# Taking the high and the low part of x in one 512-column matmul, in a one-core transformer block

## The chip, the core and the metric

The kernel runs on one core of a Trainium2 chip. The metric is device time in microseconds for one launch: 1659.37 us is the median of three runs of the kernel before (1657.81 to 1660.90 us).

The core has five engines that run side by side and wait for one another through semaphores: PE (TensorE, the matrix products; "PEld" in the profile is its loading of weights), DVE (VectorE), ACT (ScalarE), POOL (GpSimd) and SP, which here only issues the loads of the large weights. A matmul holds one operand in the array (the weights, 128 rows by up to 128 columns) and streams the other past it (the moving operand, up to 512 columns). Its sums go to PSUM, a memory of 8 banks of 512 floats on each of 128 partitions; DVE and ACT read it and write to SBUF. That reading is called eviction below.

## What is computed

One block of a network on 256 tokens of 2048 channels, in float32 throughout. Cut to the matrix products with the large weights:

```python
h = rms_norm(x);  u = h @ w_in                       # 2048 x 6000, a little over
y = concat(ssd_mixer(u[...]), rwkv7_mixer(u[...]))   # two recurrent mixers
x = x + y @ w_out                                    # 2048 x 2048
h = rms_norm(x);  m = rms_norm(mem)                  # 256 memory tokens
x = x + softmax((h @ wq) (m @ wk).T) (m @ wv) @ wo   # 4 heads of 512
h = rms_norm(x);  x = x + square(relu(h @ w1)) @ w2  # 2048 x 8192 x 2048
return rms_norm(x)
```

## The kernel before

**Products in three parts.** TensorE takes float32 operands in one pass if they are rounded to a shorter mantissa (the type fp32r). To keep float32 accuracy the kernel splits each operand into a high part `hi` (rounded) and a low part `lo` (the rest, rounded), by `split`: ACT writes `hi`, DVE writes `lo = src - hi`. A product w·x then is `whi·xhi + whi·xlo + wlo·xhi`, three matmuls that add into the same PSUM columns.

**A unit.** All large products but one (`wv`) go through `unit`. A unit is 128 output channels (112 and 96 in the first two): 16 tiles of 128 input channels, in two halves of 8. The weights are the operand held in the array, x transposed is the moving one, with 256 tokens as its columns. For each half, lines 197 and 198 run the 8 pairs `whi·xhi`, `whi·xlo` in turn, and line 204 then runs the 8 `wlo·xhi`. That makes 48 matmuls of 256 columns a unit, each with its own weight load; the sum takes 256 of the 512 floats of a bank. There are 240 units: 48 of `w_in`, 16 each of `wk`, `w_out`, `wq` and `wo`, 64 of `w1` and 64 of `w2`. The product with `wv` (lines 856, 858, 859) is laid out the other way about: memory tokens are held in the array and 512 columns of the weights move.

**Weights.** SP issues the load of a half (512 KB) ahead of its use, ACT splits off its `hi` (`L161`, 128x1024), DVE its `lo` (`L162`). In the MLP whole units are loaded (1 MB) and there are two more pairs of buffers for the parts (`wvb` and `wZ` in the names of the rows).

**Eviction.** PSUM is used through two pools: `acc`, three banks for units, and `sm`, five for everything else. One instruction evicts a unit: a DVE product with the norm's factor (`L320`, `L374`, `L379`, `L841`, `L977`), a DVE addition to the residual (`L871`), or a `split` straight from PSUM for the queries.

**Work beside the units.** The two mixers, the memory's norm and the attention are written as generators. `unit` calls `beside` after each quarter of a unit, and `beside` lets them issue some of their instructions. While the 48 units of `w_in` and the first ones of `wk` run, DVE and ACT thus also compute the mixers. The framework's scheduler then fixes the order on each engine; an engine works off its order strictly, an instruction that waits holds up all behind it.

**x in parts.** The split inputs are pairs of tiles, `Ahi`, `Alo` and `Bhi`, `Blo` in the rows (`pair_tiles`), each 16 x 256 floats on a partition. `Bhi` and `Blo` also hold x itself at first, then tensors of the mixers (`ar`, `bk`), then the memory.

Of the kernel before, what the change touches and what calls it, by code (L numbers as in the profile page):

```python
# [18 lines left out]
P = 128  # L19
# [9 lines left out]
# Per-channel vectors, one column of 128 channels each.  # L29
# [12 lines left out]
# Width of each unit of w_in, in the order in which the units are worked on.  # L42
# [28 lines left out]
def trunk(ctx, tc, xT, memT, cpack, w_in, w2, a2, g2, w_out, wq, wk, wv, wo, w1, w2f, outT):  # L71
# [28 lines left out]
    # tri[s, l] = 1 where s <= l; mask[(hh, uv, s), (ar, t)]: s < t for a, s <= t for r.  # L100
# [7 lines left out]
    # Rows for the two parts of a number, so that one product sums them and spreads them over partitions.  # L108
# [18 lines left out]
    # Loads the table that the first norm needs.  # L127
# [14 lines left out]
    # Halves of what goes into a tanh that stands for a sigmoid, and 1 - mu.  # L142
# [48 lines left out]
    def unit(w_u, m, xh, xl, raws=(None, None), interleaved=False):  # L191
        """PSUM [m, T] = (2048 rows of weights, m columns)ᵀ · xᵀ."""
        halves = [load_half(w_u[:, h * 8 * m:(h + 1) * 8 * m], (8, m), raws[h]) for h in range(2)]
        ps = acc.tile([P, 512], F32, name="acc")
        for h, (wh, wl) in enumerate(halves):
            for j in range(8):
                mm(ps[:m, :T], wh[:, j], xh[:, 8 * h + j], start=h + j == 0, stop=False)  # L197
                mm(ps[:m, :T], wh[:, j], xl[:, 8 * h + j], start=False, stop=False)  # L198
                if interleaved:
                    mm(ps[:m, :T], wl[:, j], xh[:, 8 * h + j], start=False, stop=h * j == 7)  # L200
                if j == 5:
                    beside(PER / 4)
            for j in range(0 if interleaved else 8):
                mm(ps[:m, :T], wl[:, j], xh[:, 8 * h + j], start=False, stop=h * j == 7)  # L204
# [16 lines left out]
    def rstd_tokens(sq, width, name):  # L221
        """[token, tile] = 1 / sqrt(sum(sq) / width + eps)."""
# [9 lines left out]
    def over_partitions(r, name, copy=True):  # L232
        """[any partition, token] from [token, tile]."""
# [11 lines left out]
    # ==== 1. norm and input projection ====  # L245
    ah, al = pair_tiles("A")
    xr = big.tile([P, KT, T], F32, name="xr", tag="Bhi")
# [5 lines left out]
    # Work beside the large products: generators that yield the unit they need  # L253
    # next (a tuple), what they have cost (a float), or for how many steps they wait for other engines (an int).
# [3 lines left out]
    def beside(part):  # L258
        """Traces a share of each stream, as far as the finished units allow."""
# [32 lines left out]
    def in_unit(n):  # L292
        m = UNITS[n][2]
        w_u = w_in[uoff[n]:uoff[n] + P * KT * m].rearrange("(p c) -> p c", p=P)
        return unit(w_u, m, ah, al, (raws[:2], (raws[2], None), (None, None))[min(n, 2)], n == 0)

    # What the first unit needs, in the order in which it needs it.
# [7 lines left out]
    for q in range(4):  # L305
        for kt in range(4 * q, 4 * q + 4):
            split(ah[:, kt], al[:, kt], xr[:, kt], col("g_mix", kt))
# [7 lines left out]
    def shifted(out, ps, name, i, m):  # L315
        """out = u + (u of the token before - u) mu, u = ps * rb; out by token, or by chunk and token."""
        u = tp.tile([P, T], F32, name="u")
        mu = col(name, i)[:m]
        with tc.high_priority():
            V.tensor_tensor(u[:m], ps[:m, :T], rb[:m], ALU.mult)  # L320
# [741 lines left out]
```

## Time and profile before

| | |
|---|---|
| median of three runs | 1659.37 us (1657.81 to 1660.90) |
| span of the profiled execution, first to last instruction | 1658.7 us |
| PE busy | 1630.8 us, 13631 matmuls |
| DVE busy | 1011.0 us, 1506 instructions |
| ACT busy | 825.0 us, 1197 instructions |
| POOL busy | 115.7 us |
| read from HBM | 277.34 MB, 169 GB/s over the span |
| mean granted TensorE clock | 0.993 of full speed |

The profiled execution's own time is its span of 1658.7 us and the little that lies around it; the page gives no other figure for it.

Matmuls are pipelined: a row's duration (0.28 us for 256 columns) includes the way through the array, and the next matmul starts long before it ends. What a matmul costs in a stream is therefore read from the distance of the starts, and a PE that is "busy" all the time is not shown by that to be at its limit. Durations of single DVE and ACT instructions overlap slightly in the same way (two of 0.42 us back to back take 0.76 us).

### The profile page before, as it was taken

The numbers are of one execution on the slowest core, as the hardware profiler recorded it, in microseconds if no ns is written. First come the engines' busy times: TensorE is split into PE (matmuls) and PEld (weight loads), VectorE is DVE, ScalarE is ACT, GpSimd is POOL, SyncE is SP. The second block draws the span as 40 slices with busy tenths as digits, with TensorE's granted clock in tenths as the row PEclk, the third lists the DMA queues.
The fourth block names the chain that finished last, engine by engine and source line by source line (L and its number), as shares of the span: only waits on it lengthen the run. The fifth ranks groups of instructions, "written<-read, shape, count | busy, mean of one in ns | idle before, by whom it ended". The sixth has DMA issues, their size and how long they took to land.

```text
span 1658.7 us, 32204 instructions
## 1 busy us (share of the span) xinstructions
PE 1630.8 (98%) x13631; PEld 1592.7 (96%) x13631; DVE 1011.0 (61%) x1506; ACT 825.0 (50%) x1197; POOL 115.7 (7%) x147
## 2 busy tenths in 40 slices
PE   7999999998999999999999999999999999999997
PEld 7999999998998889999999999999999999999997
DVE  6876697889676446655666555455544554455543
ACT  5674445685455445445545554344433543345553
POOL 1011112112000002100011000000000000000011
PEclk9999999999999999999999999999999999999998
DMA  6554455353456665554665555555555555555551
GB/s 190 170 162 146 131 181 161 102 162 105 150 151 209 195 189 184 178 166 141 229 186 164 170 189 181 178 181 188 190 180 178 181 186 190 180 179 181 186 189 55
DMA packets 61040, 282.56 MB, mean 170 GB/s; under 512 B 7456, under 2 KB 8352, under 8 KB 44512
## 3 DMA queue, kind: packets, MB, share of 16 engines
q1 hardware_dynamic: 57312, 272.39, 50.8%
q0 software_dynamic: 3008, 6.03, 1.2%
q8 instruction: 106, 1.74, 0.4%
q10 hardware_dynamic: 576, 2.10, 0.4%
q14 instruction: 38, 0.31, 0.1%
HBM read 277.34 MB, written 3.15 MB: 169 GB/s over the span
## 4 chain that ended last, share of the span: by engine, by line
PE 94%; issue 3%; DVE 1%; DMA 1%; ACT 0%; POOL 0%; SPq 0%; DVEq 0%; POOLq 0%; ACTq 0%
PE acc L197 27%; PE acc L204 27%; PE acc L198 27%; PE acc L858 2%; PE acc L856 2%; PE acc L859 2%; PE sm L478 1%; PE sm L599 1%; DMA raw<-in 1%; PE sm L226 1%; PE sm L896 0%; PE sm L898 0%; PE sm L897 0%; PE sm L395 0%; PE sm L587 0%
## 5 line engine op out<-in xcount | busy, mean ns | idle before, releaser
L197 PE MATMUL acc<-Ahi,hi 128*128 128x256 f32 (+2 forms) x1792 | 450.1, 288 | 8.4 <-ACT hi L161 8.4
L198 PE MATMUL acc<-Alo,hi 128*128 128x256 f32 (+2 forms) x1792 | 445.7, 285 | 1.4 <-DVE Alo L165 1.4
L161 ACT CAST hi<-raw 128x1024 fp32r<-128x1024 f32 (+1 forms) x256 | 267.7, 1046 | 284.8 <-PE acc L198 173.1
L162 DVE TENSOR_TENSOR lo<-raw,hi 128x1024 fp32r<-128x1024 f32 (+1 forms) x256 | 312.0, 1219 | 131.5 <-ACT hi L161 121.8
L197 PEld LDWEIGHTS acc<-Ahi,hi 128*128 128x128 f32 (+2 forms) x1792 | 345.1, 193 | 10.7 <-ACT hi L161 8.4
L198 PEld LDWEIGHTS acc<-Alo,hi 128*128 128x128 f32 (+2 forms) x1792 | 345.2, 193 | 2.8 <-DVE Alo L165 2.1
L197 PE MATMUL acc<-Bhi,hi 128*128 128x256 f32 x1024 | 253.1, 284 | 0.0
L204 PE MATMUL acc<-Ahi,lo 128*128 128x256 f32 (+1 forms) x1776 | 252.5, 284 | 0.0
L198 PE MATMUL acc<-Blo,hi 128*128 128x256 f32 x1024 | 252.2, 283 | 0.0
L204 PEld LDWEIGHTS acc<-Ahi,lo 128*128 128x128 f32 (+1 forms) x1776 | 230.4, 192 | 0.4
L197 PEld LDWEIGHTS acc<-Bhi,hi 128*128 128x128 f32 x1024 | 196.5, 192 | 1.0 <-issue 0.2
L198 PEld LDWEIGHTS acc<-Blo,hi 128*128 128x128 f32 x1024 | 196.6, 192 | 0.1
L204 PE MATMUL acc<-Bhi,lo 128*128 128x256 f32 x1024 | 146.7, 285 | 0.0
L219 POOL TENSOR_TENSOR sq<-sq,t 128x256 f32<-128x256 f32 x50 | 54.8, 1096 | 1181.8 <-ACT t L218 1176.8
L204 PEld LDWEIGHTS acc<-Bhi,lo 128*128 128x128 f32 x1024 | 133.5, 193 | 0.8 <-issue 0.6
L871 DVE TENSOR_TENSOR x<-x,acc 128x256 f32<-128x256 f32 x96 | 40.4, 421 | 150.4 <-PE acc L204 150.4
L198 PE MATMUL acc<-Blo,wvb 128*128 128x256 f32 x512 | 125.7, 283 | 0.0
L197 PE MATMUL acc<-Bhi,wvb 128*128 128x256 f32 x512 | 125.7, 283 | 0.0
L197 PE MATMUL acc<-Ahi,wvb 128*128 128x256 f32 x512 | 125.6, 283 | 0.0
L198 PE MATMUL acc<-Alo,wvb 128*128 128x256 f32 x512 | 125.6, 283 | 0.0
L161 ACT CAST hi<-wK 128x1024 fp32r<-128x1024 f32 x64 | 67.0, 1047 | 92.2 <-PE acc L198 92.2
L161 ACT CAST hi<-wV 128x1024 fp32r<-128x1024 f32 x64 | 67.0, 1047 | 92.0 <-PE acc L198 92.0
(316 smaller groups left out, 2455.2 us busy)
## 6 DMA issues: line engine op xcount, KB each, us to landing
raw<-in SPq DMA_DIRECT2D x252, 512.0 KB, 3.9
wK<-in SPq DMA_DIRECT2D x64, 1024.0 KB, 4.8
wV<-in SPq DMA_DIRECT2D x64, 1024.0 KB, 4.9
xr<-in SPq DMA_DIRECT2D x4, 512.0 KB, 9.1
mr<-in POOLq DMA_DIRECT2D x4, 512.0 KB, 5.6
x<-in ACTq DMA_DIRECT2D x4, 512.0 KB, 5.9
out<-x SPq DMA_DIRECT2D x7, 256.0 KB, 2.4
u<-in POOLq DMA_DIRECT2D x8, 128.0 KB, 3.2
```

Source lines behind the costliest of these rows:

```text
L161: nc.scalar.copy(hi, src)
L162: V.tensor_tensor(lo, src, hi.bitcast(F32), ALU.subtract)
L197: mm(ps[:m, :T], wh[:, j], xh[:, 8 * h + j], start=h + j == 0, stop=False)
L198: mm(ps[:m, :T], wh[:, j], xl[:, 8 * h + j], start=False, stop=False)
L204: mm(ps[:m, :T], wl[:, j], xh[:, 8 * h + j], start=False, stop=h * j == 7)
L219: nc.gpsimd.tensor_tensor(sq, sq, t, ALU.add)
L226: mm(ps[:, i:i + 1], q[:, i * P:(i + 1) * P], ones[:, 0:1], start=k == 0, stop=k == len(sq) - 1)
L478: mm(o[:, c * 64:c * 64 + 64], bk[HH[hh], p, c].rearrange("p k t -> p (k t)"), ar[HH[hh], p, c].rearrange("p k t -> p (k t)"), start=True, ...
L856: mm(pss[i], mh[:, kt, tk], wl[:, j], start=False, stop=kt == KT - 1)
L858: mm(pss[i], mh[:, kt, tk], wh[:, j], start=kt == 0, stop=False)
L859: mm(pss[i], ml[:, kt, tk], wh[:, j], start=False, stop=False)
L871: V.tensor_tensor(x2[:, i], x2[:, i], ps[:, :T], ALU.add)
```

## The change

`unit` takes x as one tile that holds both parts, `x[:, 0]` high and `x[:, 1]` low. The pair `whi·xhi`, `whi·xlo` becomes one matmul of 512 columns: its moving operand is `x[:, :, kt]`, two runs of 256 floats that lie 16 x 256 floats apart, and its output is the whole bank, `whi·xhi` in the left half and `whi·xlo` in the right. The `wlo·xhi` matmuls add to the left half as before. At eviction the halves are summed: `joined` lets ACT copy the right half to SBUF (tile `j`, one buffer) and DVE add the left half to it, and what follows reads `j`; `residual` adds both halves to x2, one after the other. `pair_tile` gives one tile of twice the size, so that `ar` and `bk` share one, too. Comments were taken out, so line numbers move.

```diff
-    def unit(w_u, m, xh, xl, raws=(None, None), interleaved=False):
+    def unit(w_u, m, x, raws=(None, None), interleaved=False):
...
         for h, (wh, wl) in enumerate(halves):
             for j in range(8):
-                mm(ps[:m, :T], wh[:, j], xh[:, 8 * h + j], start=h + j == 0, stop=False)
-                mm(ps[:m, :T], wh[:, j], xl[:, 8 * h + j], start=False, stop=False)
+                kt = 8 * h + j
+                mm(ps[:m].rearrange("p (s t) -> p s t", s=2), wh[:, j], x[:, :, kt], start=kt == 0, stop=False)
                 if interleaved:
-                    mm(ps[:m, :T], wl[:, j], xh[:, 8 * h + j], start=False, stop=h * j == 7)
+                    mm(ps[:m, :T], wl[:, j], x[:, 0, kt], start=False, stop=kt == 15)
...
             for j in range(0 if interleaved else 8):
-                mm(ps[:m, :T], wl[:, j], xh[:, 8 * h + j], start=False, stop=h * j == 7)
+                mm(ps[:m, :T], wl[:, j], x[:, 0, 8 * h + j], start=False, stop=h * j == 7)
...
-    def pair_tiles(tag):
-        return (big.tile([P, KT, T], F32R, name=f"{tag}hi", tag=f"{tag}hi"),
-                big.tile([P, KT, T], F32R, name=f"{tag}lo", tag=f"{tag}lo"))
+    def joined(ps, m=P):
+        t = tp.tile([P, T], F32, name="j", bufs=1)
+        with tc.high_priority():
+            nc.scalar.copy(t[:m], ps[:m, T:])
+            V.tensor_tensor(t[:m], t[:m], ps[:m, :T], ALU.add)
+        return t
+
+    def pair_tile(tag):
+        return big.tile([P, 2, KT, T], F32R, name=f"{tag}pair", tag=tag)
...
-                V.tensor_tensor(xc[:, i], ps[:, :T], rb, ALU.mult)
+                V.tensor_tensor(xc[:, i], joined(ps), rb, ALU.mult)
...
         with tc.high_priority():
-            V.tensor_tensor(x2[:, i], x2[:, i], ps[:, :T], ALU.add)
+            for s in range(2):
+                V.tensor_tensor(x2[:, i], x2[:, i], ps[:, s * T:(s + 1) * T], ALU.add)
...
-            V.scalar_tensor_tensor(t, ps[:, :T], 0.0, rbf, ALU.max, ALU.mult)
+            V.scalar_tensor_tensor(t, joined(ps), 0.0, rbf, ALU.max, ALU.mult)
             act(t, t, AF.Square)
-            split(fh[:, j], fl[:, j], t)
+            split(f_[:, 0, j], f_[:, 1, j], t)
```

On PE, where one half of a unit of `w2` ends and the next begins (`Ahi`, `Alo`, later `Apair`, is x; `hi`, `lo`, `wvb`, `wZ` are parts of weights), there stood before:

```order
L197 MATMUL acc<-Ahi,hi 128x256
L198 MATMUL acc<-Alo,hi 128x256
L204 MATMUL acc<-Ahi,lo 128x256 [waits DVE_49]
L204 MATMUL acc<-Ahi,lo 128x256 x7
L197 MATMUL acc<-Ahi,wvb 128x256 [waits Activation_49]
L198 MATMUL acc<-Alo,wvb 128x256
```

In the same place of the changed kernel stand:

```order
L199 MATMUL acc<-Apair,wvb 128x512 [waits DVE_49,Activation_49]
L199 MATMUL acc<-Apair,wvb 128x512 x7
L205 MATMUL acc<-Apair,wZ_8949 128x256 [waits DVE_49]
L205 MATMUL acc<-Apair,wZ_8949 128x256 x7
L199 MATMUL acc<-Apair,hi 128x512 [waits Activation_49]
```

Sixteen matmuls of 256 columns have become eight of 512; the eight of 256 columns with the low part of the weights are left. The first matmul of a unit now waits for two engines, since both ACT and DVE read the bank that it writes.

On DVE, at the eviction of a unit of `w1` (its norm's product, `t<-acc,rb`, and the split of the result), there stood before:

```order
L162 TENSOR_TENSOR Alo<-t,Ahi 128x256 [waits Activation_49]
L162 TENSOR_TENSOR lo<-wK_10477,hi 128x1024 [waits DVE_49,DMAHW5_49,PE_49,Activation_49]
L977 SCALAR_TENSOR_TENSOR t<-acc,rb 128x256 [waits PE_49]
L162 TENSOR_TENSOR wZ_10476<-wK_10477,wvb 128x1024 [waits DVE_49,Activation_49]
L162 TENSOR_TENSOR Alo<-t,Ahi 128x256 [waits Activation_49]
```

There now stand:

```order
L162 TENSOR_TENSOR lo<-wV_8951,hi 128x1024 [waits PE_49,Activation_49]
L214 TENSOR_TENSOR j<-j,acc 128x256 [waits DVE_49,Activation_49]
L987 SCALAR_TENSOR_TENSOR t<-j,rb 128x256 [waits DVE_49]
L162 TENSOR_TENSOR lo<-wK_8950,hi 128x1024 [waits DMAHW1_49,PE_49,Activation_49]
L162 TENSOR_TENSOR Apair<-t,Apair 128x256 [waits Activation_49]
```

One addition of 128x256 more, and it waits for ACT, whose copy of the right half (`L213 COPY j<-acc`, new in ACT's order) waits for PE.

On PE, near the end of the mixers, where the memory's first units (`Bhi`, later `Bpair`, is the memory in parts) run beside the transposes and the gate (`L631`, `L639`, later `L639`, `L647`), there stood before:

```order
L631 MATMUL sm<-ident,rx 128x128 [waits DVE_49]
L631 MATMUL sm<-ident,rx 128x128 x2
L197 MATMUL acc<-Bhi,hi 128x256
L197 MATMUL acc<-Bhi,hi 128x256 [waits Activation_49]
L198 MATMUL acc<-Blo,hi 128x256
L197 MATMUL acc<-Bhi,hi 128x256
L639 MATMUL sm<-pg,u 128x256 [waits DMASW2_49,Activation_49]
L639 MATMUL sm<-pg,u 128x256
L631 MATMUL sm<-ident,rx 128x128 [waits Activation_49]
```

There now stand:

```order
L199 MATMUL acc<-Bpair,hi 128x512 [waits DVE_49]
L205 MATMUL acc<-Bpair,lo 128x256
L199 MATMUL acc<-Bpair,hi 128x512 [waits DVE_49] x4
L199 MATMUL acc<-Bpair,hi 128x512 [waits Activation_49]
L199 MATMUL acc<-Bpair,hi 128x512 x4
L639 MATMUL sm<-ident,rx 128x128 [waits DVE_49]
L639 MATMUL sm<-ident,rx 128x128 x2
L647 MATMUL sm<-pg,u 128x256 [waits DMASW2_49,Activation_49]
```

More of the memory's first two units now stands ahead of the transposes, and each of its matmuls needs both parts of its tile, where `whi·xhi` needed only the high one.

## Rows read from the trace of the kernel before

**Rows 1.** The page: busy time and share of each engine, then the chain by engine.
```profile
PE 1630.8 (98%) x13631; PEld 1592.7 (96%) x13631; DVE 1011.0 (61%) x1506; ACT 825.0 (50%) x1197; POOL 115.7 (7%) x147
...
PE 94%; issue 3%; DVE 1%; DMA 1%; ACT 0%; POOL 0%; SPq 0%; DVEq 0%; POOLq 0%; ACTq 0%
```

**Rows 2.** Waits of PE: who waited for whom, total us, times, longest us.
```profile
PE acc L197 <- ACT hi L161: 8.4, 1, 8.4
PE sm L729 <- DVE vb L640: 2.4, 1, 2.4
PE sm L639 <- DMA u<-in: 1.7, 2, 0.9
PE sm L226 <- POOL sq L219: 1.6, 2, 0.8
```

**Rows 3.** Busy us (count) of each engine by stretch, then granted clock, DMA share, GB/s.
```profile
33.00:240.00 207.00, 206.51 (x1787) 201.85 (x1786) 157.89 (x284) 115.97 (x186) 23.26 (x32) 0.99 0.52 156
240.00:320.00 80.00, 80.00 (x911) 76.34 (x911) 63.86 (x129) 44.80 (x79) 13.78 (x25) 1.00 0.45 134
320.00:380.00 60.00, 59.94 (x719) 56.45 (x718) 53.55 (x96) 44.59 (x82) 9.26 (x13) 1.00 0.48 153
380.00:412.00 32.00, 27.28 (x182) 24.79 (x181) 29.96 (x57) 19.74 (x34) 8.00 (x8) 0.95 0.30 92
...
912.00:1640.00 728.00, 728.00 (x6069) 728.00 (x6069) 371.95 (x442) 329.09 (x408) 14.44 (x13) 1.00 0.52 177
```

**Rows 4.** PE in order of time, two halves of `w2` meeting: start, duration, line, count.
```profile
1000.11 1.12 PE L204 MATMUL acc<-Bhi,lo 128*128 128x256 f32 x8
1001.07 0.28 PE L197 MATMUL acc<-Ahi,hi 128*128 128x256 f32 x1
1001.19 0.28 PE L198 MATMUL acc<-Alo,hi 128*128 128x256 f32 x1
```

**Rows 5.** PE in order of time, the product with `wv`, 512 columns.
```profile
528.78 1.07 PE L856 MATMUL acc<-lo,Bhi 128*128 128x512 f32 x4
529.69 0.39 PE L858 MATMUL acc<-hi,Bhi 128*128 128x512 f32 x1
...
531.50 1.07 PE L856 MATMUL acc<-lo,Bhi 128*128 128x512 f32 x4
```

**Rows 6.** PE groups by line and form: mean ns of one, idle before.
```profile
L204 PE MATMUL acc<-Ahi,lo 128*128 128x256 f32 (+1 forms) x1776 | 252.5, 284 | 0.0
L204 PE MATMUL acc<-Bhi,lo 128*128 128x256 f32 x1024 | 146.7, 285 | 0.0
L204 PE MATMUL acc<-Bhi,wZ 128*128 128x256 f32 x512 | 71.9, 283 | 0.0
L204 PE MATMUL acc<-Ahi,wZ 128*128 128x256 f32 x512 | 71.9, 283 | 0.0
```

**Rows 7.** PE in order of time, 28 to 30 us.
```profile
28.29 0.41 PE L197 MATMUL acc<-Ahi,hi 128*96 128x256 f32 x1
...
29.79 0.41 PE L198 MATMUL acc<-Alo,hi 128*96 128x256 f32 x1
```

**Rows 8.** As rows 3, the stretch from 28 us.
```profile
28.00:33.00 5.00, 5.00 (x28) 5.00 (x29) 0.68 (x4) 1.50 (x3) 0.00 (x0) 0.58 0.12 47
```

**Rows 9.** DVE and ACT groups by form: count, busy us, mean ns, idle before.
```profile
L871 DVE TENSOR_TENSOR x<-x,acc 128x256 f32<-128x256 f32 x96 | 40.4, 421 | 150.4 <-PE acc L204 150.4
L573 ACT COPY t<-sm 128x256 f32<-128x256 f32 x8 | 3.0, 372 | 2.2 <-PE sm L571 2.1
```

**Rows 10.** DVE in order of time, evictions of `w1` and (back to back) `wk`.
```profile
1542.71 0.42 DVE L977 SCALAR_TENSOR_TENSOR t<-acc,rb 128x256 f32<-128x256 f32 x1 [1.54 <-PE acc L204]
1543.05 1.22 DVE L162 TENSOR_TENSOR lo<-wV,hi 128x1024 fp32r<-128x1024 f32 x1
1544.18 0.42 DVE L162 TENSOR_TENSOR Alo<-t,Ahi 128x256 fp32r<-128x256 f32 x1
...
422.68 0.76 DVE L841 TENSOR_TENSOR kx<-acc,rb 128x256 f32<-128x256 f32 x2 [1.45 <-issue]
```

**Rows 11.** DVE in order of time, the last two evictions of `w_in`.
```profile
379.71 0.42 DVE L374 TENSOR_TENSOR xc<-acc,rb 128x256 f32<-128x256 f32 x1
...
386.74 0.42 DVE L374 TENSOR_TENSOR xc<-acc,rb 128x256 f32<-128x256 f32 x1
```

**Rows 12.** As rows 3, the first ten us of the crowded stretch.
```profile
380.00:390.00 10.00, 9.54 (x76) 9.09 (x74) 10.00 (x20) 7.26 (x12) 1.12 (x2) 1.00 0.47 142
```

**Rows 13.** As rows 3, instructions on the tile `acc` alone, without POOL.
```profile
240.00:320.00 80.00, 56.67 (x441) 53.68 (x441) 3.80 (x9) 0.00 (x0) 1.00 0.45 134
320.00:380.00 60.00, 40.25 (x307) 37.30 (x305) 2.84 (x7) 0.00 (x0) 1.00 0.48 153
380.00:412.00 32.00, 16.86 (x117) 15.54 (x118) 0.56 (x2) 0.00 (x0) 0.95 0.30 92
```

More of the change, by code (lines that the diff above doesn't have):

```diff
@@ L243, in over_partitions @@
         return b
-    ah, al = pair_tiles("A")
-    xr = big.tile([P, KT, T], F32, name="xr", tag="Bhi")
+    a_ = pair_tile("A")
+    xr = big.tile([P, KT, T], F32, name="xr", tag="B")
     uoff, off = [], 0
@@ L294, in in_unit @@
         w_u = w_in[uoff[n]:uoff[n] + P * KT * m].rearrange("(p c) -> p c", p=P)
-        return unit(w_u, m, ah, al, (raws[:2], (raws[2], None), (None, None))[min(n, 2)], n == 0)
+        return unit(w_u, m, a_, (raws[:2], (raws[2], None), (None, None))[min(n, 2)], n == 0)
     raws = []
@@ L335, in trunk @@
     H16 = slice(96, 112)
-    ar = big.tile([P, 8, NCH, 2, C], F32, name="ar", tag="Bhi")
-    bk = big.tile([P, 8, NCH, 2, C], F32, name="bk", tag="Blo")
+    arbk = big.tile([P, 2, 8, NCH, 2, C], F32, name="arbk", tag="B")
+    ar, bk = arbk[:, 0], arbk[:, 1]
     rx = big.tile([P, 16 * T + 8 * NCH], F32, name="rx", tag="X16")
@@ L642, in normed @@
         yield ("xbc", 7)
[L644 removed]
+        y2.append(pair_tile("A"))
         for p in range(8):
[L646 removed]
+            split(y2[0][:, 0, 8 + p], y2[0][:, 1, 8 + p], vb[:, p])
             yield 0.4
@@ L835, in trunk @@
     finish(s_mem)
-    mh, ml, rtm, rbm = m2
+    m_, rtm, rbm = m2
+    mh, ml = m_[:, 0], m_[:, 1]
     kx = big.tile([P, KT, T], F32, name="kx", tag="K16")
     for i in range(16):
-        ps = unit(wk[i], P, mh, ml)
+        ps = unit(wk[i], P, m_)
         with tc.high_priority():
-            V.tensor_tensor(kx[:, i], ps[:, :T], rbm, ALU.mult)
+            V.tensor_tensor(kx[:, i], joined(ps), rbm, ALU.mult)
     finish(s_mix)
-    yh, yl = y2
+    y_, = y2
     vx = big.tile([P, 2, D], F32, name="vx", tag="V16")
@@ L870, in residual @@
         with tc.high_priority():
-            V.tensor_tensor(x2[:, i], x2[:, i], ps[:, :T], ALU.add)
+            for s in range(2):
+                V.tensor_tensor(x2[:, i], x2[:, i], ps[:, s * T:(s + 1) * T], ALU.add)
         if sq is not None:
             square_into(sq, x2[:, i], i == 0)
-    hh_, hl_ = pair_tiles("B")
+    h_ = pair_tile("B")
     sqx = tp.tile([P, T], F32, name="sq")
     for i in range(16):
-        ps = unit(w_out[i], P, yh, yl)
+        ps = unit(w_out[i], P, y_)
         residual(ps, i, sqx)
-        split(hh_[:, i], hl_[:, i], x2[:, i], col("g_x", i))
+        split(h_[:, 0, i], h_[:, 1, i], x2[:, i], col("g_x", i))
     rtx = rstd_tokens([sqx], D, "x")
     V.tensor_scalar(rtx, rtx, 512 ** -0.5, None, ALU.mult)
-    oh, ol = pair_tiles("A")
+    o_ = pair_tile("A")
     qp = big.tile([P, 2, 4, T], F32R, name="qp", tag="Z8")
@@ L942, in trunk @@
     for i in range(16):
-        ps = unit(wq[i], P, hh_, hl_)
+        ps = unit(wq[i], P, h_)
         while i % 4 == 0 and i and ("s", i // 4 - 1) not in done:
@@ L946, in trunk @@
         with tc.high_priority():
-            split(qp[:, 0, i % 4], qp[:, 1, i % 4], ps[:, :T])
+            split(qp[:, 0, i % 4], qp[:, 1, i % 4], joined(ps))
         done.add(("q", i))
     finish(s_att)
-    hh_, hl_ = pair_tiles("B")
+    h_ = pair_tile("B")
     sqx = tp.tile([P, T], F32, name="sq")
     for i in range(16):
-        ps = unit(wo[i], P, oh, ol)
+        ps = unit(wo[i], P, o_)
         residual(ps, i, sqx)
-        split(hh_[:, i], hl_[:, i], x2[:, i], col("g_ffn", i))
+        split(h_[:, 0, i], h_[:, 1, i], x2[:, i], col("g_ffn", i))
     rbf = over_partitions(rstd_tokens([sqx], D, "ffn"), "ffn")
@@ L972, in trunk @@
     for q in range(4):
-        fh, fl = pair_tiles("A")
+        f_ = pair_tile("A")
         for j in range(16):
-            ps = unit(w1[16 * q + j], P, hh_, hl_, whole(w1[16 * q + j]))
+            ps = unit(w1[16 * q + j], P, h_, whole(w1[16 * q + j]))
             t = temp()
-            V.scalar_tensor_tensor(t, ps[:, :T], 0.0, rbf, ALU.max, ALU.mult)
+            V.scalar_tensor_tensor(t, joined(ps), 0.0, rbf, ALU.max, ALU.mult)
             act(t, t, AF.Square)
-            split(fh[:, j], fl[:, j], t)
+            split(f_[:, 0, j], f_[:, 1, j], t)
         for i in range(16):
-            ps = unit(w2f[q, i], P, fh, fl, whole(w2f[q, i]))
+            ps = unit(w2f[q, i], P, f_, whole(w2f[q, i]))
             residual(ps, i, sqx if q == 3 and i < KT - 1 else None)
```

22 lines of the change are left out of this document (10 added, 12 removed).

## The prediction

> **What bounds the kernel now.** I first read the busy shares and the chain of work that ended last [rows 1]. PE is busy for 98% of the span and carries 94% of the chain; DVE carries 1%. A pipelined PE can look busy while it waits, so I then read whom PE waited for [rows 2]: 8.4 us before the first matmul, and after that nothing over 2.4 us. The table of stretches says where another engine comes near [rows 3]. In the MLP, from 912 to 1640 us, DVE is busy for 372 of 728 us. Beside the mixers it climbs: 80% from 240 to 320 us, 89% from 320 to 380 us, and 29.96 of 32 us from 380 to 412 us, the one stretch where PE is plainly idle (27.28 of 32). So the kernel is a stream of matmuls almost from end to end, with one place of 32 us where DVE sets the pace.
>
> **What the change does to the stream.** The price of one matmul is the distance of starts. Eight of 256 columns start within 0.96 us, so one costs 0.120 us [rows 4]. At 2.4 GHz, 256 columns are 0.1067 us, which leaves 0.0133 us that isn't columns. Where 512 columns move, 12 matmuls (4 of L856, 8 of L858 and L859) take from 528.78 to 531.50 us, 0.2267 us each [rows 5]; 512 columns at 2.4 GHz are 0.2133 us, and again 0.0133 us is left over. The extra time thus belongs to the matmul with its weight load, not to its columns. A pair costs 2 x 0.120 = 0.240 us now and would cost 0.2267 us as one matmul: 0.0133 us less. The pairs are as many as the matmuls with the low part of the weights: 1776 + 1024 + 512 + 512 [rows 6], and 16 in the first unit, 3840 in all. That is 3840 x 0.0133 = 51.2 us, or 0.213 us in a unit of 5.76 us. The number of columns stays the same. In the new stream a half holds eight matmuls of 512 columns and then eight of 256, so each regime is one that the trace shows, with only two changes between them.
>
> At the lower clock nothing is saved. From 28.29 to 29.79 us seven matmuls start 0.214 us apart [rows 7], which is 256 columns at 1.2 GHz with nothing left over; the granted clock there is 0.58 on the mean, between the two levels, after PE had run a row of one-column sums [rows 8]. Of the 28 matmuls in that stretch about 11 pairs are concerned, and I take as many again for the start and for the dip around 410 us: 24 x 0.0133 = 0.3 us.
>
> The Trainium skill, in "TensorE: Matmul & The Clock Gate", section "Wait — 56ns, not 53.3ns?", knows such a fixed cost per matmul, hidden at 1.2 GHz and seen only at 2.4 GHz, and the trace agrees with that much. But the page puts it at about 2.5 ns, and by that figure the 3840 pairs would give 9.6 us; the trace has 13.3 ns in both forms, so the sum goes by the trace.
>
> **What is not in the trace.** No large matmul of the kernel before reads its moving operand in two runs. The bounds come from the nearest rows: if the seam costs nothing, the price is that of 512 columns in one run, 0.2267 us; if the second run costs as much as a matmul of its own, it is 0.240 us as now. Neither end excludes something dearer. I take the first, since the runs are long (256 floats) and there is one seam in 512 columns.
>
> **What is added.** 144 units (48 of `w_in`, 16 of `wk`, 16 of `wq`, 64 of `w1`) get an ACT copy and a DVE addition; the 96 residual units get a second DVE addition. A DVE addition from PSUM is 0.42 us, an ACT copy of this size 0.37 us [rows 9]. That makes 240 x 0.42 = 101 us more on DVE and 144 x 0.37 = 53 us more on ACT. Where that lands decides what it costs:
>
> MLP, and the other units after 412 us: nothing. DVE gets 128 x 0.42 = 54 us on its 372 us there and has 728 - 128 x 0.213 = 701 us, 61%. What hides it is the stream of matmuls: three banks are in rotation, so a bank may stay unread for two units, some 11 us. The last unit of `w1` is the tight place, because the first unit of `w2` needs its result for its last tile. Today the result is there 1.9 us after the eviction starts (1542.71 to 1544.60 us) [rows 10]. With the copy and the addition that becomes about 2.7 us; the new unit comes to that tile after 15 x 0.2267 + 8 x 0.120 = 4.36 us. If that cover went, each of the four places would cost what is over.
>
> 380 to 412 us: no gain, and a loss. DVE is late there already. Its 117 unit matmuls [rows 13] hold 39 pairs, 0.5 us that isn't saved, and two more evictions [rows 11] add 2 x 0.42 = 0.8 us to a full engine: 1.3 us.
>
> 320 to 380 us: seven evictions [rows 13] add 2.9 us, and 307 / 3 = 102 pairs take 1.4 us away: DVE would be busy for 56.5 of 58.6 us, 96%. The lower bound is nothing, as from 320 to 380 us now, where PE hardly idles at 89%. The upper bound is that DVE can't get above its present 89%: 56.5 / 0.8925 = 63.3 us, 4.7 us more than 58.6. The nearest row is the one right behind, where DVE is full and PE idles for 0.46 of 10 us [rows 12]; by its 4.6% I take 2.7 us.
>
> 240 to 320 us: nine evictions add 3.8 us, 147 pairs take 2.0 us: 67.6 of 78.0 us, 87%, less than the 89% at which PE did not wait. I take nothing; if DVE stayed at 80%, it would be 84.7 us, 6.7 us over.
>
> Ends of phases: the second addition to the residual costs 0.76 - 0.42 = 0.34 us [rows 10]. It is hidden in 93 of 96 units. It is not where PE waits for the sum of squares, two times 0.8 us [rows 2], nor behind the last unit: 3 x 0.34 = 1.0 us.
>
> The larger tile for `ar` and `bk` and the two waits at a unit's start I cost at nothing: the first is claimed while PE still works on the first units, the second is for reads two units old.
>
> **The sum.** 51.2 - 0.3 - 1.3 - 2.7 - 1.0 = 45.9 us. The profiled execution spans 1658.7 us, 0.7 us under the median of the runs, which I take to be what lies around the span. 1658.7 + 0.7 - 45.9 = 1613.5 us.
>
> **Rivals.**
>
> *DVE takes over beside the mixers.* The additions lie on an engine that works strictly in order and also feeds PE with the low parts of the weights; behind a late addition, which waits for ACT's copy, stands the next `lo`. If DVE can't exceed its present shares from 240 to 380 us, that costs 6.7 + 4.7 = 11.4 us in place of 2.7 us: 1622.2 us. For it speak the 89% and 94%; against it that PE waited for no `lo` after the first unit [rows 2].
>
> *The seam costs a start.* If the second run of the moving operand begins with the same 0.0133 us, a pair costs 0.240 us as before, the 51.2 us vanish and the additions stay: 1613.5 + 51.2 = 1664.7 us, slower than before. It decides from 45.9 / 3840 = 0.0120 us a seam on. Nothing in the rows shows it; that columns cost the same in both lengths speaks for a plain stream of columns. The Trainium skill, "Advanced Engine Details and Errata", section "Memory Cachelines", says that any non-contiguous pattern in PSUM slows matmuls markedly, and that SBUF wants consecutive accesses on a 16-byte line. No row here shows either; the output is one run of a whole bank and the operand's runs fill their lines, so by that section the seam should be cheap.
>
> *Only a part of the fixed time goes.* If half of the 0.0133 us stays, because a long matmul between short ones does not find its weights as early as it does among its like, the gain is smaller by 25.6 us: 1639.1 us. Rows 5 speak against it, since each matmul there has a weight load of its own and keeps the same 0.0133 us. By the 2.5 ns of the page named above it would be 1659.4 - 9.6 + 5.3 = 1655.1 us.
>
> That the instruction is cut back into two is excluded: the order shows one matmul of 128x512.
>
> **How the numbers follow.** The forecast has 0.72; its own range is 1606 to 1620 us (nothing lost beside the mixers, or twice what I took). DVE beside the mixers has 0.17, the seam 0.05, the part of the fixed time 0.03; 0.03 is left for what I don't see. The range of 8 in 10 runs from 1603 to 1628 us: above to the DVE case with both stretches and the dense one behind them, below 5 us under a sum without any loss, for waits that go with 3840 instructions less. A change of under 0.2% (3.3 us) could not be told from none. Faster: 0.72 + 0.17 + 0.03 + 0.02 = 0.94. The seam case spreads around 1664.7 us, 0.04 of it slower and 0.01 within the bound; what I don't see gives the last 0.01 to no change.
>
> **What would show it.** In the profile after: 9791 matmuls on PE; in the MLP a unit every 5.55 us, 512-column starts 0.227 us apart and 256-column ones 0.120 us; if the former stand 0.240 us apart, the seam is the cause. ACT near 878 us and DVE near 1110 us busy. PE idle for some 7 us from 320 to 412 us where it was 4.8; if PE waits for `lo` (now L162) by more than 5 us in total, the DVE rival is right. The forecast is wrong if the units of the MLP are not 0.2 us shorter, or if the time beside the mixers grows.

## The result: faster, by less than half of what was forecast

The changed kernel takes 1638.99 us, the median of four runs (1635.12 to 1642.31), against 1658.59 for the kernel before beside it: a ratio of 0.9883, 95% interval 0.9863 to 0.9903. The forecast was 1613.5 us with a range up to 1628. Some 25 us of gain are missing by the medians. The profiled execution is the quickest of the four, 1635.12 us with a span of 1633.4 and a mean granted clock of 0.994, where the others have 0.991 (which is worth 0.003 x 1638 = 4.9 us at most). Against it 1658.7 - 1633.4 = 25.3 us came, where 45.9 were due, so 20.6 us are to be found in the trace.

The page of the changed kernel: busy time of each engine, then the chain, to be held against [rows 1].

```profile
PE 1599.0 (98%) x9791; PEld 1383.5 (85%) x9791; DVE 1096.9 (67%) x1746; ACT 852.6 (52%) x1341; POOL 127.2 (8%) x147
...
PE 93%; DVE 4%; ACT 1%; issue 1%; DMA 1%; POOL 0%; SPq 0%; DVEq 0%; POOLq 0%; ACTq 0%
```

The count of matmuls is as forecast, and DVE's load is near its number (1110 expected); ACT's is 25 us under the 878 expected. PE is again 98% busy and carries 93% of the chain; the page's only hint of a loss is DVE's share of the chain, 4% where it was 1%. So the first thing to read is the pace of PE in the MLP. The changed kernel's PE in order of time (start, duration, line, count), to be held against [rows 4, 5]:

```profile
1001.65 2.00 PE L199 MATMUL acc<-Apair,hi 128*128 128x512 f32 x8
1003.49 1.11 PE L205 MATMUL acc<-Apair,lo 128*128 128x256 f32 x8
1004.44 2.00 PE L199 MATMUL acc<-Apair,hi 128*128 128x512 f32 x8
1006.28 1.11 PE L205 MATMUL acc<-Apair,lo 128*128 128x256 f32 x8
1007.24 1.09 PE L199 MATMUL acc<-Apair,wvb 128*128 128x512 f32 x4
```

A unit takes 1007.24 - 1001.65 = 5.59 us, where 5.55 was forecast. Eight 512-column matmuls take 1.84 us, not 8 x 0.2267 = 1.81; eight of 256 take 0.95, not 0.96. Taken for every unit, the missing 0.04 us make 240 x 0.039 = 9.4 us.

Then the landmarks. The first addition to the residual by DVE, which ends the first unit of `w_out`, started at 609.73 us before and comes here:

```profile
611.94 0.42 DVE L881 TENSOR_TENSOR x<-x,acc 128x256 f32<-128x256 f32 x1 [1.44 <-PE acc L205]
```

The first 64 units should have brought it forward by 9.4 us (13.7 less the terms for the clock and for the crowded stretches); it is 2.2 us later. From there to the last residual the kernel gained 28.3 us (1037.1 before, 1008.8 after), with 36.5 forecast. So the miss has three places: 9.4 us in the pace of all units (2.5 of them in the first 64, 6.9 in the other 176), another 9.0 us in the first 610 us, and some 2 us at the ends of phases and in the tail. The 9.0 us are flattered: before its first residual this execution was granted half clock (1.2 of 2.4 GHz) for 6.8 us, the one of the kernel before for 13.7 us. With equal half clock (contig below, the same kernel in pace and time) the first residual comes at 613.9.

The stretches of the changed kernel (columns as in [rows 3]):

```profile
33.00:240.00 207.00, 204.30 (x1310) 177.25 (x1309) 165.58 (x311) 121.22 (x215) 20.70 (x32) 0.98 0.50 157
240.00:320.00 80.00, 79.33 (x795) 68.42 (x794) 66.93 (x136) 47.09 (x87) 13.65 (x25) 1.00 0.44 134
320.00:380.00 60.00, 59.96 (x576) 48.94 (x576) 52.13 (x100) 44.17 (x88) 7.62 (x14) 1.00 0.46 148
380.00:412.00 32.00, 24.33 (x126) 18.64 (x125) 30.26 (x58) 20.25 (x35) 10.24 (x7) 1.00 0.29 91
```

From 380 to 412 us DVE is as full as before (29.96, now 30.26) and PE does less: 24.33 in place of 27.28 us. From 33 to 240 us PE idles for 2.7 us where it idled for 0.5. Whom PE waited for, to be held against [rows 2]:

```profile
PE sm L234 <- POOL sq L227: 2.2, 2, 1.1
PE sm L699 <- DVE s L684: 2.1, 1, 2.1
PE sm L737 <- DVE cbm L738: 2.0, 1, 2.0
PE acc L199 <- DVE Apair L165: 1.5, 2, 1.2
...
PE acc L205 <- DVE lo L162: 1.3, 1, 1.3
PE sm L647 <- DMA u<-in: 1.3, 1, 1.3
PE sm L647 <- DVE Apair L162: 1.2, 1, 1.2
```

The waits are many and short, most of them on DVE. The wait for `s` (transposes of dt) is new and comes at 58 us; behind it the clock falls. PE in order of time there, then the stretch from 62 us (granted clock in the third column from the end):

```profile
57.22 0.81 PE L199 MATMUL acc<-Apair,hi 128*128 128x512 f32 x2
60.13 0.20 PE L699 MATMUL sm<-ident,s 16*128 16x16 f32 x1 [2.09 <-DVE s L684]
...
62.29 3.37 PE L199 MATMUL acc<-Apair,hi 128*128 128x512 f32 x8
65.50 0.76 PE L205 MATMUL acc<-Apair,lo 128*128 128x256 f32 x5
```
```profile
62.00:64.00 2.00, 2.00 (x6) 1.61 (x7) 1.60 (x3) 1.42 (x4) 0.17 (x1) 0.50 0.00 0
```

PE's eight 512-column matmuls take 65.50 - 62.29 = 3.21 us, not 1.84. "Busy" PE at half clock hides 1.4 us that no wait shows.

### The profile page after: what moved, and what is told of

It reads as the page before. It is cut to its first block, busy times and chain, and to the rows that moved or that the text cites. A ratio compares the mean times of both kernels' runs of the same rounds, so it can differ in the third digit from the quotient of the medians.

```text
span 1633.4 us, 25004 instructions
## 1 busy us (share of the span) xinstructions
PE 1599.0 (98%) x9791; PEld 1383.5 (85%) x9791; DVE 1096.9 (67%) x1746; ACT 852.6 (52%) x1341; POOL 127.2 (8%) x147
## 4 chain that ended last, share of the span: by engine, by line
PE 93%; DVE 4%; ACT 1%; issue 1%; DMA 1%; POOL 0%; SPq 0%; DVEq 0%; POOLq 0%; ACTq 0%
PE acc L199 52%; PE acc L205 27%; PE acc L867 2%; PE acc L865 2%; PE acc L868 2%; DVE lo L162 1%; PE sm L486 1%; PE sm L607 1%; PE sm L595 1%; DMA raw<-in 1%; PE sm L565 1%; PE sm L234 0%; PE sm L906 0%; PE sm L908 0%; PE sm L907 0%
## 5 line engine op out<-in xcount | busy, mean ns | idle before, releaser
L199 PE MATMUL acc<-Apair,hi 128*128 128x512 f32 (+2 forms) x1792 | 468.7, 399 | 9.3 <-ACT hi L161 7.8
L199 PEld LDWEIGHTS acc<-Apair,hi 128*128 128x128 f32 (+2 forms) x1792 | 323.5, 190 | 69.6 <-ACT hi L161 7.8
L199 PE MATMUL acc<-Bpair,hi 128*128 128x512 f32 x1024 | 263.1, 395 | 0.5 <-DVE Bpair L165 0.3
L205 PEld LDWEIGHTS acc<-Apair,lo 128*128 128x128 f32 (+1 forms) x1776 | 243.5, 190 | 18.7
L205 PE MATMUL acc<-Apair,lo 128*128 128x256 f32 (+1 forms) x1776 | 253.3, 283 | 0.0
L199 PEld LDWEIGHTS acc<-Bpair,hi 128*128 128x128 f32 x1024 | 182.8, 189 | 35.2 <-DVE Bpair L165 1.5
L205 PEld LDWEIGHTS acc<-Bpair,lo 128*128 128x128 f32 x1024 | 140.4, 190 | 13.0 <-DVE lo L162 1.7
L205 PE MATMUL acc<-Bpair,lo 128*128 128x256 f32 x1024 | 145.9, 283 | 1.3 <-DVE lo L162 1.3
L199 PE MATMUL acc<-Apair,wvb 128*128 128x512 f32 x512 | 129.1, 393 | 0.0
L199 PE MATMUL acc<-Bpair,wvb 128*128 128x512 f32 x512 | 128.7, 393 | 0.0
```

The source lines that it names most:

```text
L199: mm(ps[:m].rearrange("p (s t) -> p s t", s=2), wh[:, j], x[:, :, kt], start=kt == 0, stop=False)
L205: mm(ps[:m, :T], wl[:, j], x[:, 0, 8 * h + j], start=False, stop=h * j == 7)
```

## Experiments

Theory at the start: the pace is lost to the seam in the moving operand (some 2.4 ns each), the first 610 us to the additions on DVE. Rivals: the pace belongs to the mixture of lengths; the front (those 610 us) is lost to the scheduler's new places for the mixers' small products, or to chance. Ratios are to the kernel before, run on the same chip. The groups of runs lie on several chips, on which the kernel before took 1656.96 to 1660.45 us, so differences between groups are good to some 3 us.

```
kernel     median us  ratio   95%              first residual (one profile)
changed    1638.99    0.9883  0.9863-0.9903    611.9
contig     1637.97    0.9883  0.9863-0.9903    613.9
leaveout   1622.32    0.9787  0.9767-0.9806    598.9
sx8        1637.38    0.9870  0.9845-0.9895    619.6
oldextra   1641.18    0.9901  0.9883-0.9919    621.1
flip       1641.27    0.9894  0.9877-0.9911    619.4
interl     1645.36    0.9917  0.9904-0.9930    614.0
copyonly   1626.95    0.9800  0.9784-0.9816    604.0
pooladd    1644.10    0.9912  0.9895-0.9928    620.4
hybrid     1629.74    0.9830  0.9809-0.9851    607.2
hybflip    1627.87    0.9823  0.9805-0.9841    604.5
lateold    1629.62    0.9829  0.9810-0.9848    608.6
short      1632.24    0.9835  0.9816-0.9854    612.7
```

The last column is that of one execution and varies by some us, among other things with stretches at half clock that come or don't; the medians decide.

**contig**: the pair in one run (the other indices of the pair tiles are turned round in the same way).
```
-        return big.tile([P, 2, KT, T], F32R, ...)
+        return big.tile([P, KT, 2, T], F32R, ...)
-                mm(ps[:m]..., wh[:, j], x[:, :, kt], ...)
+                mm(ps[:m]..., wh[:, j], x[:, kt], ...)
```


> Only the layout of the pair tiles changes: x's high and low 256 columns of a k-tile lie side by side, so the 512-column matmul reads one run of 512 floats in place of two runs 16 KB apart. Order of all engines' instructions as in the changed kernel. Theory A (the second run of the operand costs some 2.4 ns for each of the 3840 matmuls): the unit of the MLP goes from 5.586 to about 5.55 us, the whole kernel gains 3840 x 2.4 ns = 9 us, about 1630 us. Rival B (the 2.4 ns belong to a matmul that fills the bank in the two-way order, or to the weights beside it, not to the layout): unit 5.586, time within 2 us of the changed kernel's.

Nothing changed, in the time or in the pace. PE of contig, in order of time:

```profile
1003.60 2.00 PE L199 MATMUL acc<-Apair,hi 128*128 128x512 f32 x8
1005.44 1.12 PE L205 MATMUL acc<-Apair,lo 128*128 128x256 f32 x8
1006.40 2.00 PE L199 MATMUL acc<-Apair,hi 128*128 128x512 f32 x8
```

1.84 and 0.96 us, as in the changed kernel (1.84 and 0.95). The seam costs nothing; my theory fell. The Trainium skill, "Advanced Engine Details and Errata", section "Memory Cachelines", gives full performance to accesses in SBUF that go on within the same line; both layouts here move long runs, and the equal pace agrees. The starts one by one then showed where the ns are: in the five 512-column matmuls behind a run of 256-column ones. In the changed kernel's run that begins at 1004.44 us (shown above) the last three are:

```profile
1005.60 0.84 PE L199 MATMUL acc<-Apair,hi 128*128 128x512 f32 x3
```

The first five starts span 1005.60 - 1004.44 = 1.16 us where 5 x 0.2267 = 1.13 was due; the last three take 1006.28 - 1005.60 = 0.68 us, which is 3 x 0.2267.

**flip**: half as many changes of length.
```
         for h, (wh, wl) in enumerate(halves):
+            for j in range(8 if h and not interleaved else 0):
+                mm(ps[:m, :T], wl[:, j], x[:, 0, 8 + j], start=False, stop=False)
...
-            for j in range(0 if interleaved else 8):
+            for j in range(0 if interleaved or h else 8):
```


> In the second half of each unit (the first unit apart) the eight 256-column matmuls stand ahead of the eight 512-column ones, so that runs of 8 and 8 become runs of 16 and 16; same matmuls, same weights. The changed kernel's trace shows five 512-column starts of 233, 236, 228, 232 and 231 ns behind a run of 256-column ones, then 226.7, and two short 256-column ones, 113 and 119 ns, behind a run of 512: 27.1 - 7.5 = 19.6 ns net for each half of a unit. Theory A (that is the price of changing from one length to the other): half the changes, MLP unit 5.586 to 5.566 us, 240 x 19.6 ns = 4.7 us less, 1634. Rival B (it belongs to the first five weights of a half, whatever stands before): unit 5.586, 1639. The scheduler's places in the first 600 us move too; the unit of the MLP decides.

PE of flip, in order of time:

```profile
1003.71 1.11 PE L207 MATMUL acc<-Apair,lo 128*128 128x256 f32 x8
1004.66 1.12 PE L198 MATMUL acc<-Apair,wZ 128*128 128x256 f32 x8
1005.62 3.82 PE L201 MATMUL acc<-Apair,wvb 128*128 128x512 f32 x16
1009.28 1.12 PE L207 MATMUL acc<-Apair,wZ 128*128 128x256 f32 x8
```

A unit is 1009.28 - 1003.71 = 5.57 us, as theory A says. In the run of 16 only the first five starts are late (233, 236, 228, 232, 231 ns), all others are 226.7. The time as a whole did not follow: the first residual came at 619.4; in the first 600 us PE now waited, among other things, for `lo` (3.2 us, eight times) and for a DMA of the recurrence (2.2 us, up to 276.7 us), with half clock from 278 to 281 us. What decides the theory is the pace, and that is confirmed.

**interl**: a change of length at every matmul (`interleaved=True` for all units).

> Every unit as the first one: a 512-column matmul, then the 256-column one of the same k-tile, sixteen times over. Theory A1 (each change of length costs 19.6 ns net, without an end): 14 more pairs of changes in a unit, 5.586 + 0.274 = 5.86 us, 66 us slower, 1705. Theory A2 (the price is a debt of some lengths that is paid off over five 512-column matmuls, so that a pair costs 233.3 + 113.3 = 346.6 ns): unit 5.546, 9.5 us faster, 1630. The first unit of the changed kernel shows pairs of 346 to 353 ns, so between 5.54 and 5.65 us.

PE of interl, in order of time:

```profile
1000.88 0.39 PE L199 MATMUL acc<-Apair,wvb 128*128 128x512 f32 x1
1001.11 0.28 PE L201 MATMUL acc<-Apair,wZ 128*128 128x256 f32 x1
1001.23 0.39 PE L199 MATMUL acc<-Apair,wvb 128*128 128x512 f32 x1
1001.46 0.28 PE L201 MATMUL acc<-Apair,wZ 128*128 128x256 f32 x1
```

A pair takes 0.353 us on the mean of the trace (235.9 + 116.9 ns), a unit 5.645. Both extremes fell: 6 ns over 346.7 for each pair, not 19.6 and not none. A change of length has a price of its own, smaller when the run behind it is short. Why the chip does so stays open. By the unit the kernel should take 240 x 0.059 = 14 us more than the changed one, 1653; it takes 1645. The first 64 units show no loss: the first residual comes at 614.0, and at 613.9 in contig, with the same half clock (13.7 us) before it. The slower pace cost nothing there, in an order that is not quite the same.

**leaveout, copyonly, short**: the eviction in `w_in` and `wk` without its two new instructions, without the addition, and with a short one.
```
     def joined(ps, m=P, front=True):
+        if front: return ps[:, :T]      # leaveout
...
             nc.scalar.copy(t[:m], ps[:m, T:])
+            if front: return ps[:, :T]      # copyonly
...
+        n = 32 if front else T      # short
...
+            if front: V.tensor_tensor(t[:m, :n], t[:m, :n], ps[:m, :n], ALU.add)
...
+        return ps[:, :T] if front else t
```


> Left out: in the 64 units of w_in and wk the right half of the bank is not read (no ACT copy, no DVE addition); matmuls as in the changed kernel. Theory A (the 64 evictions' added DVE and ACT work beside the mixers is what ate the gain of the first 600 us): the first residual of w_out comes at about 600 us in place of 611.9, the kernel takes about 1627 us. Rival B (the loss there comes from where the scheduler puts the mixers' small products among longer matmuls): the first residual stays above 608, time above 1635.

> Left out: the DVE addition of the halves in the 64 units of w_in and wk; ACT's copy of the right half stays (nothing reads it). Without both the kernel took 1622.3, with both 1639. Theory A (DVE's 64 x 0.414 us of additions, beside a DVE that is the pace of the mixers, is the price): 1622 to 1626, first residual of w_out about 601. Rival B (ACT's copies cost as much): 1630 or more.

> Left out: in the 64 units of w_in and wk the DVE addition takes 32 columns in place of 256 (some 0.1 us in place of 0.414), and what follows reads the left half; ACT's copy is whole. One more DVE instruction in each eviction, as in the changed kernel, with a quarter of its time. Without the addition (copyonly) 1627, with the whole one 1639. Theory A (its time on DVE is the price): 1627 + 12 x 0.1 / 0.414 = 1630. Rival B (one more instruction with its waits, whatever its length, and the places that the scheduler finds around it): 1636 or more.

Without both 1622.3, with ACT's copy 1627.0, with everything 1639.0. The additions cost 12 us by the medians, 14 by the ratios. The copies cost 4.6 us by the medians and 2 by the ratios, and the intervals of leaveout and copyonly overlap, so that may be nothing. leaveout ended below its theory A (1627), and copyonly above its own (1622 to 1626) but far from its rival. The short addition took longer than I had put down; DVE of short, by form:

```profile
L215 DVE TENSOR_TENSOR j<-j,acc 128x256 f32<-128x256 f32 x80 | 33.1, 414 | 1.6 <-ACT j L213 1.6
L214 DVE TENSOR_TENSOR j<-j,acc 128x32 f32<-128x32 f32 x62 | 11.3, 182 | 0.3
```

With 182 ns theory A gives 1627 + 12 x 182 / 414 = 1632.3, and 1632.24 was measured: as far as runs that are good to 3 us tell, the price goes with the time on DVE, not with the instruction. That it met the tenth is luck. What the additions hold up is seen in copyonly, from 380 to 412 us (columns as above):

```profile
380.00:412.00 32.00, 29.89 (x175) 24.70 (x174) 30.83 (x61) 22.17 (x39) 7.11 (x6) 1.00 0.40 118
```

DVE is full there with or without the additions, and PE is 29.89 us busy in place of 24.33. PE's eight waits in this stretch sum to 7.6 us in the changed kernel, its three in copyonly to 2.0. The two kernels are not at quite the same work then (copyonly begins its 49th unit at 382.0 us, the changed kernel at 383.2), so this shows the kind of the loss and not its size; the table below has that.

**oldextra**: the three old matmuls in the front, with as many added instructions (copy of the left half, maximum of it and itself).

> In the 64 units of w_in and wk the three 256-column matmuls of the kernel before, all into the left half; at eviction an ACT copy of it and a DVE maximum of the copy and the same half are added, as many instructions of the same sizes as the changed kernel's copy and addition. Everything after as in the changed kernel. Theory A (the eviction's added work costs some 13 us there whatever the matmuls): first residual of w_out about 620 us, end about 1647. Rival B (the added work is hidden when the matmuls are the old ones; the loss comes with the new order): first residual about 610, end about 1637.

First residual of oldextra:

```profile
621.14 0.42 DVE L885 TENSOR_TENSOR x<-x,acc 128x256 f32<-128x256 f32 x1 [1.44 <-PE acc L209]
```

11.4 us later than in the kernel before, on the same matmuls. The end, 1641, lies between the two forecasts, but the clean measure came with hybrid below, which is this kernel without the added work: 1641.2 - 1629.7 = 11.5 us (11.8 by the ratios). The added work costs that by itself, and rival B (it comes with the new matmuls' order) falls for that part.

**sx8**: the wait at 58 us taken away (`'x': 8` for `'x': 4` in `STEPS`).

> The five 16-wide transposes of dt are put eight quarters of a unit after their chain's start in place of four, so that they stand some 11 us later in TensorE's order; nothing else moves. Theory A (the wait of 2.1 us at 58 us and the half clock behind it cost the end what they cost there, 4 to 5 us): no wait of TensorE for s at that place, full clock from 62 to 66 us, 1634 us. Rival B (the work beside the products is paced by DVE's chain up to 380 us, so time won at 60 us is waited away there): wait and half clock gone too, but the eviction times at 380 us and the end as in the changed kernel, 1639.

Inconclusive. The wait shrank to 1.3 us, but in the profiled execution the clock fell all the same, from 70 to 73 us, and again from 275 to 282 us, about a wait of 3.7 us for a DMA of the recurrence that ended at 275.2 us; the six runs lie between 1629.7 and 1642.6 us.

**pooladd**: the addition moved to POOL.
```
+                nc.scalar.copy(t[:m], ps[:m, T:])
+                nc.scalar.copy(to, ps[:m, :T])
+                nc.gpsimd.tensor_tensor(to, to, t[:m], ALU.add)
```


> In the 64 units of w_in and wk ACT copies both halves of the bank out (two copies) and POOL adds them (some 1.1 us each); DVE is left with the one multiplication of the kernel before. Same result. Theory A (DVE's time is the price): most of the 13 us come back, 1624 to 1630. Rival B (ACT's second copy, POOL's longer way or the port that POOL and DVE share take it back): 1637 or more.

Rival B: 1644. PE's waits in pooladd, the two longest sums:

```profile
PE acc L199 <- ACT hi L161: 10.0, 6, 7.7
PE sm L584 <- DVE wx L564: 3.1, 2, 2.1
```

ACT with a second copy comes late with the weights' high parts (six waits, where the changed kernel has two; 7.7 of the 10.0 us are the wait at the start), and the recurrence waits for DVE all the same. DVE itself was not relieved: up to the first residual it is busy for longer than in copyonly with as many instructions. Pooladd, then copyonly:

```profile
0.00:620.36 620.36, 593.15 (x3960) 496.03 (x3961) 456.95 (x810) 370.81 (x677) 131.86 (x167) 0.99 0.49 157
0.00:603.95 603.95, 588.02 (x3960) 496.53 (x3961) 446.40 (x810) 354.17 (x613) 66.89 (x103) 0.99 0.50 161
```

How the loss divides among the three causes that rival B names is not shown.

**hybrid, hybflip, lateold**: the old three matmuls and one-instruction eviction in `w_in` and `wk`; the same with flip in the other 176 units; the same as hybrid, but units 0 to 27 in the new form.

> The 64 units of w_in and wk as in the kernel before (three 256-column matmuls into the left half, one DVE operation at eviction), the other 176 as in the changed kernel. Theory A (in the first 600 us the added DVE work eats the shorter matmuls' gain and more): w_out's first residual as in the kernel before (610 us), then 176 units x 0.174 us less what the ends of the phases lose (28 us in the changed kernel's trace): about 1630. Rival B (the loss in the changed kernel's first 600 us was chance of the clock and the DMAs): 1637 to 1640, no better than the changed kernel.

> As hybrid, and in the second half of each of the 176 units the eight 256-column matmuls stand ahead of the 512-column ones. Theory A (19.6 ns for each pair of changes of length): 176 x 19.6 ns = 3.4 us below hybrid, about 1627. Rival B (the runs of flip lost elsewhere because of lo being wanted earlier, in all phases): no better than hybrid.

> Units 0 to 27 (up to 225 us) as in the changed kernel, units 28 to 47 and wk as in the kernel before, the rest as in the changed kernel. Theory A (the price of the added DVE work falls where the later mixers run beside, from 225 to 515 us): 2 to 5 us below hybrid, 1625 to 1628. Rival B (as much of it falls in the first 225 us): at or above hybrid, 1630 or more.

hybrid met its number, 1629.74 for 1630: 9 us better than the changed kernel (8.8 by the ratios) with 64 units undone. First residual, then in hybflip:

```profile
607.24 0.42 DVE L885 TENSOR_TENSOR x<-x,acc 128x256 f32<-128x256 f32 x1 [1.44 <-PE acc L209]
```
```profile
604.54 0.88 DVE L888 TENSOR_TENSOR x<-x,acc 128x256 f32<-128x256 f32 x2 [1.45 <-PE acc L206]
```

hybflip is the best of those that leave nothing out and beats both kernels, 1627.87 us, ratio 0.9823 (0.9805 to 0.9841). Its interval overlaps with hybrid's, so the medians can't tell the two apart; from first to last residual it gained 1.7 us (1008.7 to 1007.1) of the 3.4 expected: 2.7 us were lost between the last residual of `w_out` and the first of `wo`, and 4.4 gained elsewhere. lateold equals hybrid: theory A asked for 2 to 5 us less, and rival B was right. 28 units in the new form should gain 28 x 0.174 = 4.9 us, and nothing came, though each interval is some 3 us wide to either side. The traces show where it went. With equal half clock so far lateold begins its ninth unit at 72.0 us and hybrid at 69.1, and the 21st at 152.3 and 151.2: 2.9 us are lost at once and then 1.8 won back, where 12 x 0.174 = 2.1 were due. What was lost at once holds a wait of PE, 2.0 us for `s`, among the five transposes of dt at 62 us. The kernel before and hybrid don't have it; but leaveout and copyonly, without any addition, wait at the same place (2.2 and 2.6 us in all), and so does oldextra with the old matmuls (2.7). Either part of the change brings it, so it is no price of the additions alone.

**Where the rest of the first 610 us went.** Three kernels, from landmark to landmark, in us: hybrid (old matmuls, nothing added), copyonly (new matmuls without the additions) and contig (the changed kernel in pace and time). PE was granted half clock for 10.2, 13.7 and 13.7 us before the 25th unit (3.5 us more of it cost 1.7), and never again before the first residual. The gain due is 0.174 us a unit.

```
                                        hybrid  copyonly  contig  gain due
to the start of the 25th unit           185.1   185.1     186.9    4.2
units 25 to 36                           79.6    77.6      77.6    2.1
units 37 to 64 (to the product with wv) 247.9   246.5     253.5    4.9
from there to the first residual         94.7    94.7      95.9    0.2
```

PE, DVE and the rest in the second of these stretches (columns as above), contig, then copyonly:

```profile
186.92:264.56 77.64, 77.64 (x509) 67.72 (x508) 68.83 (x150) 39.14 (x60) 10.65 (x16) 1.00 0.54 169
185.14:262.79 77.65, 77.65 (x508) 67.72 (x507) 65.01 (x135) 39.25 (x60) 9.54 (x14) 1.00 0.56 179
```

There the additions cost nothing, though DVE is 89% busy with them (68.83 of 77.64 us), and the shorter matmuls gain what they should. In the third stretch, where the mixers end, the new matmuls gain 1.4 us of the 4.9 due even without the additions, and the additions cost 7.0 us on top. Of the 10.0 us between the first residuals of contig and copyonly, 1.8 fall in the first stretch, none in the second, 7.0 in the third and 1.2 in the fourth.

## Why the prediction was wrong

What held: the fixed 13.3 ns of a matmul goes with it (512-column starts are 226.7 ns apart outside the five late ones, and the 176 units behind the front gained 28 us); the seam is free, as assumed without a row for it; the MLP hides all that was added; PE idles for 7.7 us from 320 to 412 us (7 forecast); PE waited for `lo` 1.3 us after the first units.

Four terms failed:

1. "Each regime is one that the trace shows, with only two changes between them": I priced the changes at nothing. They cost 27.1 - 7.5 = 19.6 ns for each half of a unit, 480 x 19.6 = 9.4 us. contig excluded the seam, flip moved the pace with the number of changes. The trace before held no run of 512 next to a run of 256 with this weight, so bounds were called for, as for the seam; the rival "only a part of the fixed time goes" has a mechanism of this kind (a long matmul between short ones), with a size (half) that was too large: 18% of the 13.3 ns, not 50%. Whether late weights are the cause, as it says, no run shows.

2. "240 to 320 us: I take nothing", 2.7 and 1.3 us beside it, and nothing elsewhere: the 64 additions cost 12 us (changed kernel less copyonly; with the copies 11.5, oldextra less hybrid), not 4. I measured DVE's room by its busy share in a stretch, and that does not tell the price: units 25 to 36 hide their additions with DVE at 89%, and units 37 to 64 pay 7.0 us for theirs. There, by the waits, PE's small products depend on what DVE still has to compute for the mixers, so an addition that goes first can make PE wait; all 64 x 0.414 = 26.5 us of additions cost 12. The DVE rival had the mechanism and nearly the price, 11.4 us, but by luck: it laid 6.7 of them on 240 to 320 us. The sign that I named for it, waits for `lo` of over 5 us, was the wrong one: in the changed kernel PE waited 1.3 us for `lo` after the first units, and otherwise for `s`, `Apair` and `cbm`, none over 2.1 us. The waits are also only a part: up to the first residual PE is idle for 19.3 us in contig and 15.9 in copyonly, 3.4 of the 10.0 us; the rest stands in time that the page calls busy.

3. "51.2 us" counts the full gain of the pairs everywhere but in 32 us and at the low clock. The front did not give it even without the additions: copyonly's first residual comes 609.7 - 604.0 = 5.8 us before that of the kernel before, with equal half clock, where 64 x 0.174 = 11.1 were due. Some 2 us of that are lost before the 25th unit, where the wait at the transposes of dt is new, and 3.5 in units 37 to 64; how much of that is DVE's chain and how much the scheduler's new order stays open. The theory that I set against the additions, new places for the mixers' small products, is thus not excluded for this part.

4. Ends of phases and the tail: 3 us in place of 1.0. POOL's sums of squares became slower, a wait of 2.2 us where it was 1.6 [rows 2], and a wait for ACT near the end takes 1.4 us where it took 0.9; the other 1 us was not traced.

In the trace of the changed kernel: 9.4 + 9.0 + 1.3 + 0.8 = 20.5 of the 20.6 us missing, the last two being what the 176 units and the tail lost beyond the pace; the 9.0 us hold the second and the third term (10.0 + 5.3 us by contig and copyonly, where 4.3 were forecast), less 3.4 us that half clock cost the kernel before and not this execution; 1.4 us are not placed. As a check on the second: leaveout has neither the copies nor the additions in the front, so the forecast for it would be 1613.5 - 4.0 + 9.4 = 1618.9, or 1621 with the 2 us of the fourth; by its ratio it takes 0.9787 x 1659.4 = 1624. The 3 us left, within the noise by themselves, go the way of the third term.

## What to carry to other kernels

When a merge of two instructions saves time on one engine and adds it on another, price each stage apart: here 176 units gained 28 us, and in the other 64 the same edit cost more than it saved, so undoing it there was worth 9 us. The busy share of a helper engine does not tell whether it has room: here work was free beside it at 89% in one stretch and dear in the next, where the main engine was waiting for its results. Test that by adding the work alone (oldextra) and by comparing landmarks of two traces stretch by stretch, at equal clock. The price of an instruction in a long uniform run is not its price next to another length.

## What the runs showed of the hardware beyond that

- Behind eight 256-column matmuls the next five of 512 columns start 233, 236, 228, 232 and 231 ns apart, then 226.7; behind a run of 512 the first two of 256 take 113 and 119 ns, then 120. In strict alternation a pair takes 353 ns.
- A moving operand in two runs of 256 floats 16 KB apart costs PE nothing against one run of 512 (eight matmuls take 1.84 us either way).
- A wait of PE of some 2 us in the stream can be followed by a stretch at 1.2 GHz that costs nearly as much again: at 62 us eight matmuls took 3.21 us in place of 1.84. It needn't be: behind the same wait of 2.0 us in contig, which ended at 63.4 us, the granted clock was 1.00 up to 70 us.
- DVE takes 182 ns for an addition of 32 columns from PSUM and 414 for 256: an eighth of the columns, 44% of the time.
- POOL's 256-column addition to the sum of squares took 1096 ns on the mean before; in the changed kernel it takes 1369. Why wasn't tried:

```profile
L227 POOL TENSOR_TENSOR sq<-sq,t 128x256 f32<-128x256 f32 x50 | 68.4, 1369 | 1137.7 <-ACT t L226 1133.2
```
